# First stage of a two-layer diffusion trunk: order of the first loads, who scales the token rows, and which modulation tiles go to TensorE

## The chip, the cores and the metric

The kernel runs on one core of a Trainium2 chip. The metric is the device time of one execution in microseconds (us). The comparison time is the median of three runs.

## What is computed

The reference is a trunk of two layers over 512 latent tokens and 256 context tokens, each 1024 wide. Layer 0 is grouped-query attention, layer 1 a pooling mixer, and each is followed by a gated ConvFFN. Only the opening of layer 0 matters here:

```python
sc, sc_ctx = silu(c), silu(c_ctx)
m  = sc     @ w_mod[0] + b_mod[0]     # 6 vectors of 1024: shift_m, scale_m, ...
mc = sc_ctx @ w_mod[0] + b_mod[0]
h  = rmsnorm(x,   g_pre) * (1 + scale_m)  + shift_m
hc = rmsnorm(ctx, g_pre) * (1 + cscale_m) + cshift_m
q, k, v = h @ w_qkv                   # context gives k and v only
```

Everything is float32 to float32 accuracy: each matmul is made of three products of a high and a low part.

## The kernel before, in words

The 1024 features are eight tiles of 128 (index j), the tokens are six tiles of 128 rows (two of context, then four of x).

**Tokens.** Lines 337 to 350: for each of the six token tiles, a DMA brings its rows, ScalarE squares them with a running sum (`rstd_row`, line 174), VectorE makes mean plus epsilon (157), GpSimd raises to the power -1/2 (151), and ScalarE multiplies the rows by the result (347). The normalised rows are `xn`.

**Modulation.** For feature tile j and v = 0 (shift) or 1 (scale), a 512 KB piece of `w_mod` lies with features on partitions. VectorE multiplies it by the row silu(c_ctx) and sums (line 329, result `cmods`), then by the row silu(c) (line 330, in place, result `mods`): four such products for each j. The rows silu(c) and silu(c_ctx) stand on every partition (`scrow`, `cscrow`) and come by a broadcast DMA and a Silu on ScalarE. Tile 5 (`PE_TILE`) is made on TensorE instead, with silu(c) as two columns (`cols`): sixteen matmuls give two rows of 256 (319), ScalarE copies these (320), two transposes turn them into columns (323), and VectorE adds the bias (324, 325). The pieces of w_mod go through four buffers in turn (`mraws`), so the fifth load waits for the first product pair.

**Loop over j** (lines 355 to 380). VectorE forms the gains `Acol` and `Acx` (359, 360). TensorE transposes tile j of the six `xn` into PSUM banks 7 (context) and 6 (x) (367). ScalarE applies gain and shift (370, 371). `split` (126 to 129) makes the high part by a ScalarE cast (128) and the low part by a VectorE subtraction (129): `hT` for x, `cT` for context, and, once for two j, `wkvh` and `wkvl` for the weights of k and v. Then eighteen matmuls (122 to 124) add the tile's share to six banks. The weights of v and k go through two buffers `raw`.

**After the loop** come the rotary tables (`fold_rope`, 387: a DMA into the slots of `cT`, then VectorE), the weights of q (`load_w`, DMA, cast, subtraction, into five pairs of buffers `whi` and `wlo`), 96 matmuls of q, `do_kv` for six token tiles, `q_done` and the attention.

**What sets the order.** The program is written as above and a planner puts the instructions of each engine into one fixed order when the program is built, by the place in the program and by what it expects to be ready. On the chip each engine runs its list in that order; a wait of one instruction holds all behind it. All DMAs are issued from one queue, that of SyncE (SP), in order too.

Of the kernel before, what the change touches and what calls it, by code (L numbers as in the profile page):

```python
# [11 lines left out]
F32 = mybir.dt.float32  # L12
F32R = mybir.dt.float32r
AF = mybir.ActivationFunctionType
ALU = mybir.AluOpType
AX = mybir.AxisListType

P = 128
D = 1024
SEQ = 512  # L20
CTX = 256
KT = D // P
TT = SEQ // P
CT = CTX // P
# [18 lines left out]
BW = BI + 2 * BE  # L43
NSLOT = 64

PE_TILE = 5


@with_exitstack
def trunk(ctx: ExitStack, tc: tile.TileContext, a, out: bass.AP):  # L50
    nc = tc.nc
# [17 lines left out]
    def bank(i):  # L69
        return bank_[i]  # L70
# [16 lines left out]
    def rows(name, i, n=2, dt=F32):  # L87
        return flat(slots(name, i, n, dt))
# [47 lines left out]
    def load_w(src, n, dst=None):  # L136
        raw = load_raw(src)
        if dst is None:
            hi = wp.tile([P, 1024], F32R, tag="whi", name="whi")
            lo = wp.tile([P, 1024], F32R, tag="wlo", name="wlo")  # L140
        else:
            hi, lo = dst
        split(hi, lo, raw)
        return tuple(z.rearrange("p (a b) -> p a b", a=n) for z in (hi, lo))

    def row_tile(name):
        return work.tile([P, D], F32, tag="row", name=name)
# [24 lines left out]
    def rstd_row(src, junk):  # L172
        ss = small.tile([P, 1], F32, tag="ss", name="ss")
        S.activation(junk, src, AF.Square, accum_out=ss)
        return rstd(ss, 1, D)
# [116 lines left out]
            done(t)  # L292


    crow = row_tile("crow")
    nc.sync.dma_start(out=crow, in_=a["c"][0].broadcast_to([P, D]))
    S.activation(scrow, crow, AF.Silu)
    nc.sync.dma_start(out=bmod, in_=a["b_mod"])
    nc.sync.dma_start(out=gcols, in_=a["gcols"])
    cscrow = rows("cscrow", 48)  # L300
    mraws = [rows(f"mraw{n}", i) for n, i in enumerate((54, 56, 58, 62))]
    first = [(v, j) for j in range(KT) for v in range(2)]
    pe_raw = []
    cols = small.tile([P, KT, 2], F32, name="cols", bufs=1)
    nc.sync.dma_start(out=cols, in_=a["ccols"])
    S.activation(cols, cols, AF.Silu)
    modrow = small.tile([2, 256], F32, name="modrow", bufs=1)

    def first_load():
        raw = mraws[-len(first) % 4]  # L310
        v, j = first.pop(0)
        if j == PE_TILE:

            nc.sync.dma_start(out=raw, in_=a["w_mod0"][v])
            pe_raw.append(raw.rearrange("p (k f) -> p k f", k=4))
            if v == 1:
                m = bank(7)[0:2, 256:512]
                for k in range(KT):
                    T.matmul(m, cols[:, k, :], pe_raw[k // 4][:, k % 4, :], start=k == 0, stop=k == KT - 1)
                S.copy(modrow, m)  # L320
                mc = bank(7)[:, 256:260]
                for w in range(2):
                    T.transpose(mc[:, 2 * w:2 * w + 2], modrow[:, w * P:(w + 1) * P], ident[0:2, 0:2])
                V.tensor_add(mods[:, 0, 0:2, j], mc[:, 0:4:2], bmod[:, 0, 0:2, j])
                V.tensor_add(cmods[:, :, j], mc[:, 1:4:2], bmod[:, 0, 0:2, j])
            return
        nc.sync.dma_start(out=raw, in_=a["w_mod"][0, v, j])
        bias = bmod[:, 0, v, j:j + 1]
        V.tensor_tensor_reduce(mjunk, raw, cscrow, 1.0, bias, ALU.mult, ALU.add, cmods[:, v, j:j + 1])
        V.tensor_tensor_reduce(raw, raw, scrow, 1.0, bias, ALU.mult, ALU.add, mods[:, 0, v, j:j + 1])  # L330

    ccrow = row_tile("ccrow")
    nc.sync.dma_start(out=ccrow, in_=a["c"][1].broadcast_to([P, D]))
    S.activation(cscrow, ccrow, AF.Silu)
    first_load()

    xnT = []
    for n in range(CT + TT):
        xn = rows(f"xn{n}", 16 + 2 * n)
        if n < CT:  # L340
            src = row_tile("cx")
            nc.sync.dma_start(out=src, in_=a["ctx"][n * P:(n + 1) * P, :])
        else:
            src = x[n - CT]
            nc.sync.dma_start(out=src, in_=a["x"][(n - CT) * P:(n - CT + 1) * P, :])
        r = rstd_row(src, xn)
        S.activation(xn, src, AF.Copy, scale=r)
        xnT.append(xn)
        if n % 2 == 1:
            first_load()  # L350

    cTs = [(slots(f"cT{n}", 44 + 2 * n, 2), slots(f"c32{n}", 52 + n, 1, F32)[:, 0, :CTX]) for n in range(2)]
    hh32 = h32.rearrange("p (n a) b -> p n (a b)", n=2)
    wkv = []
    for j in range(KT):
        while first and first[0][1] <= j + 1:
            first_load()
        js = slice(j, j + 1)
        V.scalar_tensor_tensor(Acol[:, 0, 0, js], mods[:, 0, 1, js], 1.0, gcols[:, 0, 0, js], op0=ALU.add, op1=ALU.mult)
        V.scalar_tensor_tensor(Acx[:, js], cmods[:, 1, js], 1.0, gcols[:, 0, 0, js], op0=ALU.add, op1=ALU.mult)  # L360
        if j % 2 == 0:
            i = 28 + 2 * j
            wkv.append(load_w(a["w_qkv"][2, j // 2], 2, (rows(f"wkvh{j}", i, dt=F32R), rows(f"wkvl{j}", i + 2, dt=F32R))))
        f = slice(j * P, (j + 1) * P)
        for n in range(CT + TT):
            tp = bank(7)[:, n * P:(n + 1) * P] if n < CT else bank(6)[:, (n - CT) * P:(n - CT + 1) * P]
# [628 lines left out]
def _layout(x, c, ctx, c_ctx, w_mod, b_mod, g_pre_mix, g_post_mix, g_pre_ffn, g_post_ffn,  # L995
# [11 lines left out]

        "w_mod": w_mod.reshape(2, D, 6, KT, P).transpose(0, 2, 3, 4, 1),

        "w_mod0": w_mod[0].reshape(2, 4, P, 6, KT, P)[:, :, :, :2, PE_TILE].transpose(0, 2, 1, 3, 4).reshape(2, P, 1024),  # L1010

        "b_mod": b_mod.reshape(2, 6, KT, P).transpose(3, 0, 1, 2),
        "g_q": g_q.reshape(1, HD),
# [34 lines left out]
```

## Time and profile before

| | us |
|---|---|
| median of three runs | 1059.87 (1058.87 to 1060.57) |
| profiled execution | 1057.91 |
| its span in the profile | 1056.1 |
| TensorE busy | 990.8 (94%) |
| VectorE busy | 747.5 (71%) |
| ScalarE busy | 512.9 (49%) |

The profiled execution is one run of its own; its span is the time from the first to the last recorded instruction, and 1.8 us lie around it. A busy engine is one with an instruction in flight, so a TensorE that is always busy need not be at its peak. The shares are means over stages that have different limits, so the opening stage is read by itself.

### The profile page before, as it was taken

The numbers are of one execution on the slowest core, as the hardware profiler recorded it, in microseconds if no ns is written. First come the engines' busy times: TensorE is split into PE (matmuls) and PEld (weight loads), VectorE is DVE, ScalarE is ACT, GpSimd is POOL, SyncE is SP. The second block draws the span as 40 slices with busy tenths as digits, with TensorE's granted clock in tenths as the row PEclk, the third lists the DMA queues.
The fourth block names the chain that finished last, engine by engine and source line by source line (L and its number), as shares of the span: only waits on it lengthen the run. The fifth ranks groups of instructions, "written<-read, shape, count | busy, mean of one in ns | idle before, by whom it ended". The sixth has DMA issues, their size and how long they took to land.

```text
span 1056.1 us, 14619 instructions
## 1 busy us (share of the span) xinstructions
PE 990.8 (94%) x5592; PEld 857.4 (81%) x5592; DVE 747.5 (71%) x1259; ACT 512.9 (49%) x989; POOL 37.4 (4%) x55
## 2 busy tenths in 40 slices
PE   0899799999979999999999999789999999999997
PEld 0667697888878888888888877788999999988885
DVE  3988788985799999554532336789799999982214
ACT  5658589955634333433321233565455555761111
POOL 2003000000000000000000001100000000000000
PEclk9999899999989999999999999899999999999999
DMA  8643422450389998223322461401223232052212
GB/s 321 195 153 96 152 93 101 157 164 19 102 291 331 335 319 296 100 100 100 100 88 93 159 194 58 160 20 61 68 93 110 91 120 81 21 170 92 98 60 80
DMA packets 40611, 143.71 MB, mean 136 GB/s; under 512 B 4906, under 2 KB 5338, under 8 KB 40540
## 3 DMA queue, kind: packets, MB, share of 16 engines
q1 hardware_dynamic: 40540, 142.77, 39.7%
q8 instruction: 44, 0.72, 0.3%
q14 instruction: 27, 0.22, 0.1%
HBM read 140.63 MB, written 2.12 MB: 135 GB/s over the span
## 4 chain that ended last, share of the span: by engine, by line
PE 75%; DVE 8%; ACT 7%; DMA 5%; issue 3%; POOL 2%; SPq 0%; DVEq 0%; ACTq 0%; POOLq 0%
PE b L122 16%; PE b L124 16%; PE b L123 16%; PE b L749 6%; PE b L751 5%; PE b L750 5%; DMA mraw<-in_w_mod 2%; POOL rr L151 2%; PE tp L541 1%; DVE wlo L129 1%; DVE mraw L186 1%; ACT whi L128 1%; DVE x L264 1%; DMA raw<-in_w_up 1%; PE sc L122 1%
## 5 line engine op out<-in xcount | busy, mean ns | idle before, releaser
L129 DVE TENSOR_TENSOR wlo<-raw,whi 128x1024 fp32r<-128x1024 f32 x105 | 128.2, 1222 | 161.3 <-ACT whi L128 161.0
L128 ACT CAST whi<-raw 128x1024 fp32r<-128x1024 f32 x105 | 110.3, 1053 | 214.7 <-PE b L124 108.3
L122 PE MATMUL b<-hT,whi 128*128 128x512 f32 (+1 forms) x480 | 174.2, 364 | 5.2 <-ACT hT L128 5.2
L123 PE MATMUL b<-hT,whi 128*128 128x512 f32 (+1 forms) x480 | 174.4, 364 | 0.6 <-DVE hT L129 0.6
L124 PE MATMUL b<-hT,wlo 128*128 128x512 f32 (+1 forms) x480 | 174.1, 363 | 0.0
L123 PE MATMUL b<-wlo,a 128*128 128x512 f32 x320 | 125.1, 391 | 0.3 <-DVE wlo L129 0.3
L122 PE MATMUL b<-whi,a 128*128 128x512 f32 x320 | 125.3, 392 | 0.0
L124 PE MATMUL b<-whi,a 128*128 128x512 f32 x320 | 124.9, 392 | 0.0
L122 PEld LDWEIGHTS b<-hT,whi 128*128 128x128 f32 x480 | 91.6, 192 | 19.2 <-ACT hT L128 5.7
L123 PEld LDWEIGHTS b<-hT,whi 128*128 128x128 f32 x480 | 91.7, 191 | 15.0 <-DVE hT L129 1.1
L186 DVE CUSTOM_DVE_ANT_0 mraw<-mraw,scrow,bmod 128x1024 f32<-128x1024 f32 x80 | 100.6, 1278 | 4.2 <-DMA mraw<-in_w_mod 4.1
L124 PEld LDWEIGHTS b<-hT,wlo 128*128 128x128 f32 x480 | 91.7, 191 | 13.8
L749 PE MATMUL b<-hT,whi 128*128 128x256 f32 x288 | 81.9, 284 | 0.1
L751 PE MATMUL b<-hT,wlo 128*128 128x256 f32 x288 | 81.5, 283 | 0.0
L750 PE MATMUL b<-hT,whi 128*128 128x256 f32 x288 | 81.4, 283 | 0.0
L151 POOL TENSOR_TENSOR rr<-rv,mhalf 128x1 f32<-128x1 f32 (+2 forms) x48 | 36.7, 767 | 1013.3 <-DVE rv L169 848.1
L123 PEld LDWEIGHTS b<-wlo,a 128*128 128x128 f32 x320 | 60.4, 189 | 13.4 <-DVE wlo L129 0.7
L122 PEld LDWEIGHTS b<-whi,a 128*128 128x128 f32 x320 | 60.3, 189 | 13.1 <-ACT h L209 0.3
L124 PEld LDWEIGHTS b<-whi,a 128*128 128x128 f32 x320 | 60.5, 189 | 12.5
L749 PEld LDWEIGHTS b<-hT,whi 128*128 128x128 f32 x288 | 55.2, 192 | 1.0 <-ACT gates L778 0.9
L750 PEld LDWEIGHTS b<-hT,whi 128*128 128x128 f32 x288 | 55.2, 192 | 0.0
L751 PEld LDWEIGHTS b<-hT,wlo 128*128 128x128 f32 x288 | 55.2, 192 | 0.0
(317 smaller groups left out, 2151.2 us busy)
## 6 DMA issues: line engine op xcount, KB each, us to landing
mraw<-in_w_mod SPq DMA_DIRECT2D x96, 512.0 KB, 4.9
raw<-in_w_up SPq DMA_DIRECT2D x52, 512.0 KB, 3.5
raw<-in_w_down SPq DMA_DIRECT2D x44, 512.0 KB, 3.4
upv<-in_w_up SPq DMA_DIRECT2D x18, 512.0 KB, 4.1
upg<-in_w_up SPq DMA_DIRECT2D x18, 512.0 KB, 3.5
raw<-in_w_qkv SPq DMA_DIRECT2D x12, 512.0 KB, 3.6
raw<-in_w_o SPq DMA_DIRECT2D x8, 512.0 KB, 3.7
x<-in_x SPq DMA_DIRECT2D x4, 512.0 KB, 9.2
```

The lines of the kernel that those rows point to most:

```text
L122: T.matmul(ps, lh, rh, start=first, stop=False)
L123: T.matmul(ps, lh, rl, start=False, stop=False)
L124: T.matmul(ps, ll, rh, start=False, stop=last)
L128: S.copy(hi, src)
L129: V.tensor_sub(lo, src, F(hi))
L151: G.tensor_tensor(r[:, :n], v, mhalf[:, :n], op=ALU.pow)
L186: V.tensor_tensor_reduce(raw, raw, scrow, 1.0, bias, ALU.mult, ALU.add, mods[:, i, v, j:j + 1])
L264: V.scalar_tensor_tensor(xc, row[:, HALVES[c]], r, xc, op0=ALU.mult, op1=ALU.add)
L541: T.transpose(tp[:, kt * P:(kt + 1) * P], p[:, (3 * n + kt) * P:(3 * n + kt + 1) * P], ident)
L749: T.matmul(ps, lhs[0], rhs[0], start=first and k == 0, stop=False, skip_group_check=True)
L750: T.matmul(ps, lhs[0], rhs[1], start=False, stop=False, skip_group_check=True)
L751: T.matmul(ps, lhs[1], rhs[0], start=False, stop=last, skip_group_check=True)
```

## The change

Six things change in the opening stage; nothing after it does.

- SyncE issues first the columns of c and the two small tables, then w_mod of tile 0, the six token tiles, the first weights of k and v, w_mod of tile 1, and only then the two broadcast rows of c, which now land directly in `scrow` and `cscrow` and get their Silu in place.
- VectorE, not ScalarE, multiplies the token rows by their scale.
- Tiles 0 and 1 are made on TensorE, tile 5 no longer. The piece of w_mod is now the stationary operand (128 x 128) and the two columns of silu(c), silu(c_ctx) the moving one, so the result comes out as columns; the ScalarE copy and the transposes go. It is 32 matmuls instead of sixteen and two transposes.
- The pieces of w_mod have sixteen buffers: four as before, ten of `whi` and `wlo`, `Grow`, and one row tile.
- VectorE's products for tile j + 2 stand in the program ahead of step j's gains and splits; before, it was tile j + 1.
- The loads of the weights of k and v stand at other places of the program.

```diff
-PE_TILE = 5
+PE_TILES = (0, 1)
+    def raw_buffer():
+        n = len(raws)
+        if n < 4:
+            return rows(f"mraw{n}", (54, 56, 58, 62)[n])
+        if n < 14:
+            tag = ("whi", "wlo")[n % 2]
+            return wp.tile([P, 1024], F32, tag=tag, name="mraw")
+        return Grow if n == 14 else row_tile("mraw")
...
+    def first_mods(j):
+        if j in PE_TILES:
+            mc = bank(7)[:, 256:260]
+            for v in range(2):
+                for k in range(KT):
+                    w = raws[j, k // 4].rearrange("p (k v f) -> p k v f", k=4, v=2)
+                    T.matmul(mc[:, 2 * v:2 * v + 2], w[:, k % 4, v, :], cols[:, k, :], start=k == 0, stop=k == KT - 1)
+            V.tensor_add(mods[:, 0, 0:2, j], mc[:, 0:4:2], bmod[:, 0, 0:2, j])
+            V.tensor_add(cmods[:, :, j], mc[:, 1:4:2], bmod[:, 0, 0:2, j])
+            return
+        for v in range(2):
+            raw, bias = raws[j, v], bmod[:, 0, v, j:j + 1]
+            V.tensor_tensor_reduce(mjunk, raw, cscrow, 1.0, bias, ALU.mult, ALU.add, cmods[:, v, j:j + 1])
+            V.tensor_tensor_reduce(raw, raw, scrow, 1.0, bias, ALU.mult, ALU.add, mods[:, 0, v, j:j + 1])
...
+    def normalise(n):
+        xn = rows(f"xn{n}", 16 + 2 * n)
+        r = rstd_row(src[n], xn)
+        V.tensor_scalar(xn, src[n], r, None, op0=ALU.mult)
+        xnT.append(xn)
...
-        S.activation(xn, src, AF.Copy, scale=r)
...
+    load_mods(0)
     for n in range(CT + TT):
+        load_x(n)
+    load_kv(0)
+    load_mods(1)
+    for n, row in enumerate((scrow, cscrow)):
+        nc.sync.dma_start(out=row, in_=a["c"][n].broadcast_to([P, D]))
+    first_mods(0)
+    for n in range(CT + TT):
+        normalise(n)
+    load_mods(2)
+    load_mods(3)
+    load_kv(1)
+    for row in (scrow, cscrow):
+        S.activation(row, row, AF.Silu)
+    first_mods(1)
+    first_mods(2)
+    load_mods(4)
+    load_mods(5)
...
     for j in range(KT):
-        while first and first[0][1] <= j + 1:
-            first_load()
+        if j == 1:
+            load_kv(2)
+            load_mods(6)
+        if j == 2:
+            load_mods(7)
+        if j == 3:
+            load_kv(3)
+        if 0 < j and j + 2 < KT:
+            first_mods(j + 2)
         js = slice(j, j + 1)
...
-        if j % 2 == 0:
-            i = 28 + 2 * j
-            wkv.append(load_w(a["w_qkv"][2, j // 2], 2, (rows(f"wkvh{j}", i, dt=F32R), rows(f"wkvl{j}", i + 2, dt=F32R))))
```

## Rows read from the trace of the kernel before

**Rows 1.** Stretches of the opening: stretch, its length, busy us by engine, clock, DMA.
```profile
0.00:31.00 31.00, 3.54 (x8) 1.38 (x8) 13.20 (x32) 18.01 (x25) 7.26 (x13) 1.00 0.71 274
31.00:66.00 35.00, 34.46 (x154) 25.33 (x155) 33.29 (x67) 16.93 (x29) 0.00 (x0) 1.00 0.62 202
66.00:77.50 11.50, 10.53 (x50) 7.91 (x49) 8.29 (x19) 7.00 (x12) 0.00 (x0) 1.00 0.55 184
77.50:100.00 22.50, 22.50 (x105) 18.25 (x105) 20.71 (x70) 18.08 (x91) 8.46 (x9) 1.00 0.23 70
```

**Rows 2.** The chain of work that ended last, opening: start, length, what.
```profile
15.13 1.54 POOL rr L151
...
16.69 1.15 ACT xn L347
...
31.35 1.22 PE b L122 x2
```

**Rows 3.** Timeline, ScalarE and VectorE: start, length, instruction, idle before and releaser.
```profile
7.17 1.06 ACT L334 ACTIVATE cscrow<-ccrow 128x1024 f32<-128x1024 f32 x1 [1.29 <-DMA ccrow<-in_c]
10.40 1.06 ACT L174 ACTIVATE xn<-cx 128x1024 f32<-128x1024 f32 x1 [2.17 <-DMA cx<-in_ctx]
...
12.87 1.28 DVE L329 CUSTOM_DVE_ANT_0 mjunk<-mraw,cscrow,bmod 128x1024 f32<-128x1024 f32 x1 [0.93 <-DMA mraw<-in_w_mod]
```

**Rows 4.** Timeline of VectorE inside the loop over j.
```profile
47.72 1.28 DVE L329 CUSTOM_DVE_ANT_0 mjunk<-mraw,cscrow,bmod 128x1024 f32<-128x1024 f32 x1
...
48.93 0.69 DVE L129 TENSOR_TENSOR hT<-h,hT 128x512 fp32r<-128x512 f32 x1
49.53 1.28 DVE L330 CUSTOM_DVE_ANT_0 mraw<-mraw,scrow,bmod 128x1024 f32<-128x1024 f32 x1
...
50.74 0.42 DVE L129 TENSOR_TENSOR cT<-c,cT 128x256 fp32r<-128x256 f32 x1
51.08 0.15 DVE L359 SCALAR_TENSOR_TENSOR Acol<-mods,gcols 128x1 f32<-128x1 f32 x1
...
51.22 1.22 DVE L129 TENSOR_TENSOR wkvl<-raw,wkvh 128x1024 fp32r<-128x1024 f32 x1
52.35 1.28 DVE L329 CUSTOM_DVE_ANT_0 mjunk<-mraw,cscrow,bmod 128x1024 f32<-128x1024 f32 x1
...
65.62 0.08 DVE L330 DVE_READ_ACCUMULATOR2_ANT mods<- 128x1 f32 x1
```

**Rows 5.** Timeline of TensorE, same loop.
```profile
53.47 2.75 PE L319 MATMUL b<-mraw,cols 128*2 128x256 f32 x12
...
61.71 0.60 PE L367 MATMUL b<-ident,xn 128*128 128x128 f32 x4
...
66.53 0.71 PE L367 MATMUL b<-ident,xn 128*128 128x128 f32 x5
...
75.83 0.72 PE L124 MATMUL b<-wkvh,hT 128*128 128x512 f32 x2 [0.97 <-DVE hT L129]
...
77.55 0.39 PE L124 MATMUL b<-wkvh,hT 128*128 128x512 f32 x1
```

**Rows 6.** Waits of VectorE from 31 to 66: total, times, longest.
```profile
DVE mods L324 <- PE b L323: 0.8, 1, 0.8
DVE cT L129 <- ACT cT L128: 0.5, 1, 0.5
DVE hT L129 <- ACT hT L128: 0.4, 1, 0.4
```

**Rows 7.** Line 241: a scaling of rows on VectorE, 512 wide: ns min/median/max.
```profile
L241 DVE TENSOR_SCALAR xn<-x,rr x6: 479/484/490, 259.7 to 277.1; 128x512 f32<-128x512 f32 x6
```

**Rows 8.** Line 367: weight loads of 128 columns: ns min/median/max.
```profile
L367 PEld LDWEIGHTS b<-ident,xn x48: 138/140/230, 13.9 to 71.8; 128*128 128x128 f32 x48
```

**Rows 9.** TensorE after an idle stretch in the attention: timeline.
```profile
119.60 0.57 PE L122 MATMUL sc<-kv,qT 128*128 128x512 f32 x1 [1.85 <-ACT p L528]
```

**Rows 10.** The stretch behind that gap; columns as in the first group.
```profile
120.00:122.00 2.00, 2.00 (x8) 1.71 (x7) 1.59 (x4) 1.93 (x4) 0.00 (x0) 0.50 0.78 252
```

More of the change, by code (lines that the diff above doesn't have):

```diff
@@ L292, in out_proj @@
             done(t)
-    crow = row_tile("crow")
-    nc.sync.dma_start(out=crow, in_=a["c"][0].broadcast_to([P, D]))
-    S.activation(scrow, crow, AF.Silu)
+    cscrow = rows("cscrow", 48)
+    cols = small.tile([P, KT, 2], F32, name="cols", bufs=1)
+    raws = {}
+    def raw_buffer():
[6 more added lines that the diff above has]
+        return Grow if n == 14 else row_tile("mraw")
@@ new lines, in load_mods @@
+    def load_mods(j):
+        for v in range(2):
+            raws[j, v] = raw_buffer()
+            src = a["w_mod0"][PE_TILES.index(j), v] if j in PE_TILES else a["w_mod"][0, v, j]
+            nc.sync.dma_start(out=raws[j, v], in_=src)
+    def first_mods(j):
[8 more added lines that the diff above has]
+            return
+        for v in range(2):
+            raw, bias = raws[j, v], bmod[:, 0, v, j:j + 1]
+            V.tensor_tensor_reduce(mjunk, raw, cscrow, 1.0, bias, ALU.mult, ALU.add, cmods[:, v, j:j + 1])
+            V.tensor_tensor_reduce(raw, raw, scrow, 1.0, bias, ALU.mult, ALU.add, mods[:, 0, v, j:j + 1])
@@ new lines, in trunk, with load_x, load_kv @@
+    src = [row_tile(f"cx{n}") for n in range(CT)] + x
+    def load_x(n):
+        nc.sync.dma_start(out=src[n], in_=a["ctx"][n * P:(n + 1) * P, :] if n < CT else a["x"][(n - CT) * P:(n - CT + 1) * P, :])
+    wkv = []
+    def load_kv(kk):
+        raw = load_raw(a["w_qkv"][2, kk])
+        i = 28 + 4 * kk
+        hi, lo = rows(f"wkvh{kk}", i, dt=F32R), rows(f"wkvl{kk}", i + 2, dt=F32R)
+        split(hi, lo, raw)
+        wkv.append(tuple(z.rearrange("p (a b) -> p a b", a=2) for z in (hi, lo)))
@@ L298, in trunk @@
+    xnT = []
+    def normalise(n):
[3 more added lines that the diff above has]
+        xnT.append(xn)
+    nc.sync.dma_start(out=cols, in_=a["ccols"])
     nc.sync.dma_start(out=bmod, in_=a["b_mod"])
     nc.sync.dma_start(out=gcols, in_=a["gcols"])
-    cscrow = rows("cscrow", 48)
-    mraws = [rows(f"mraw{n}", i) for n, i in enumerate((54, 56, 58, 62))]
-    first = [(v, j) for j in range(KT) for v in range(2)]
@@ L303, in trunk @@
-    pe_raw = []
-    cols = small.tile([P, KT, 2], F32, name="cols", bufs=1)
-    nc.sync.dma_start(out=cols, in_=a["ccols"])
-    S.activation(cols, cols, AF.Silu)
[L307 to L330, printed above, removed]
@@ L332, in trunk @@
-    ccrow = row_tile("ccrow")
-    nc.sync.dma_start(out=ccrow, in_=a["c"][1].broadcast_to([P, D]))
-    S.activation(cscrow, ccrow, AF.Silu)
-    first_load()
-    xnT = []
-    for n in range(CT + TT):
[L339 to L346, printed above, removed]
-        S.activation(xn, src, AF.Copy, scale=r)
-        xnT.append(xn)
-        if n % 2 == 1:
-            first_load()
+    S.activation(cols, cols, AF.Silu)
@@ L353, in trunk @@
     hh32 = h32.rearrange("p (n a) b -> p n (a b)", n=2)
-    wkv = []
     for j in range(KT):
-        while first and first[0][1] <= j + 1:
-            first_load()
+        if j == 1:
[7 more added lines that the diff above has]
+            first_mods(j + 2)
         js = slice(j, j + 1)
@@ L1008, in _layout @@
         "w_mod": w_mod.reshape(2, D, 6, KT, P).transpose(0, 2, 3, 4, 1),
-        "w_mod0": w_mod[0].reshape(2, 4, P, 6, KT, P)[:, :, :, :2, PE_TILE].transpose(0, 2, 1, 3, 4).reshape(2, P, 1024),
+        "w_mod0": w_mod[0].reshape(2, 4, P, 6, KT, P)[:, :, :, :2, list(PE_TILES)]
+        .transpose(4, 0, 2, 1, 3, 5).reshape(len(PE_TILES), 2, P, 1024),
         "b_mod": b_mod.reshape(2, 6, KT, P).transpose(3, 0, 1, 2),
```

## The prediction

> **What bounds the kernel now.** I read four views, from coarse to fine. The stretches first: they show whose engine is late where. Up to 31 us TensorE is nearly idle (3.54 us busy) while ScalarE has the most work, 18.01; from 31 to 66 both TensorE (34.46 of 35.00) and VectorE (33.29) are full; from 66 to 77.5 VectorE has air (8.29 of 11.50) and TensorE works off what is left; from there to 100 TensorE is full again [rows 1]. Then the chain of waits, which tells why TensorE starts late: the chain runs from token tile to token tile through ScalarE's square, GpSimd's power (up to 1.54) and ScalarE's scaling (1.15), since the scaling of one tile stands on ScalarE ahead of the square of the next, and the first matmul of k and v comes at 31.35 [rows 2]. So the opening has two bounds: a ScalarE and GpSimd chain to 31, then TensorE, with VectorE a hair behind it. The last matmul of the loop over j starts at 77.55 [rows 5]; behind it come q and the attention, which have no fixed date. What the loop's end gains, the kernel gains, unless the end of another engine is later.
>
> The timelines give the prices. A step of the loop costs TensorE 66.53 - 61.71 = 4.82 us [rows 5]. VectorE's costs are start to start: a product 48.93 - 47.72 = 1.21, the low part of x 49.53 - 48.93 = 0.60, of context 0.34, a pair of gains 51.22 - 51.08 = 0.14, the low part of a weight 52.35 - 51.22 = 1.13 [rows 4].
>
> **The loads.** The fourth 512 KB transfer had landed at 10.40 and the sixth at 12.87, so 1.24 us apiece, the queue being full [rows 3]. The same three small tables still stand ahead of these. After the change x's last tile is the eighth instead of the eleventh: 12.87 + 2 x 1.24 = 15.3. The row of c_ctx is the thirteenth: 21.5; its Silu takes 1.06 [rows 3]; the first piece of tile 2 is the fourteenth, 22.8. Hence VectorE's first product starts at 22.8, where it had started its third at 12.87 before. The later pieces come at twice the rate at which VectorE takes them (two pieces in 2.5 us, four products in 4.84), so with sixteen buffers no later product waits for a DMA. The small moves of the k and v loads on SyncE's queue cost nothing while that lead lasts; the third one waits for a `raw` buffer with tiles 6 and 7 behind it, but tile 6 lands by 12.87 + 19 x 1.24 = 36.4 and is due after sixteen products, past 42. Without the lead they would cost a transfer each, 1.24.
>
> **The token rows.** ScalarE's scaling, six of 1.15, goes [rows 2]; VectorE's is not in the trace at this width. Half the width took 0.48 [rows 7]: between that and twice it, 0.96; I take 0.96, the whole amount of work at the known rate. All six lie before 22.8, when VectorE has nothing else, so they cost nothing; uncovered they would be 5.8. The last tile is ready by 15.3 + 1.06 + 1.54 + 0.96 = 18.9, some 10 us before the old date. TensorE can begin step 0 near 21 instead of 31.35.
>
> **Modulation on TensorE.** Sixteen matmuls inside the old loop go: twelve took 2.75, so 3.7 in all, on the engine that was late [rows 5]. The 32 new ones each load 128 columns of weights and move two. No row has that shape; a load of 128 columns took 0.14 to 0.23 [rows 8], so 4.5 to 7.4, and less than nothing is not possible since none of it existed. I take 4.5, from the median. Tile 0's half runs when TensorE is idle, tile 1's at about 19 to 23, before TensorE has work for long; as shown next TensorE waits for VectorE in mid-loop, so they hide there. Two waits are new: VectorE's bias addition for tile 1 waits for these matmuls, with all products queued behind it (the pieces land at 19.1, the half takes 2.3 to 3.7, so it is done at 21.4 to 22.8, in time for 22.8); and step 0's context transposes, which write the same bank 7, wait for that addition, with no loss as long as TensorE has air. VectorE does four products less, 4.8.
>
> **Where VectorE becomes the bound.** Its products for j + 2 now stand in the program ahead of step j's splits. The old trace shows how the order turns out: behind the first product of a pair one or two other operations get in (the second of the pair works on the same piece in place), here hT; between pairs come operations that stand earlier in the program, or any when a piece is missing, as cT, the gains and a weight did before 52.35 [rows 4]. All seven pairs that began between 40 and 65 have something in between. With all pieces in place pairs follow without a gap, so hT of step j, needed by TensorE, ends up inside the last pair of tile j + 2. For hT of step 5 that is the second pair of tile 7. Ahead of it lie: 23 products, 27.8; cT of steps 0 to 4, 1.7; hT of 1 to 4, 2.4; three weights, 3.4; four pairs of gains, 0.6. From 22.8 that ends at 58.7, and hT itself (0.69) at 59.4. Then TensorE has steps 5, 6 and 7 before it: 3 x 4.82 = 14.5, so the loop ends at 73.9 where it ended at 77.8 (77.55 and one more matmul's 0.2). That is 3.9 us. Before 59 TensorE waits about 1.1 per step (VectorE gives a step every 4 x 1.21 + 0.60 + 0.34 + 0.14 = 5.9).
>
> VectorE's own waits in the old loop were 1.7: 0.8 for tile 5's transposes, which go, and 0.9 for ScalarE's casts [rows 6]. I charge 0.9 again (bounds 0 and 1.7). **Sum: 3.0 us off**, between 2.2 and 3.9. VectorE is not late behind it: its last product ends near 60.9 where it ended at 65.7 [rows 4], 4.8 earlier. The rotary tables keep their distance to the end of the loop, for they wait for cT's slots.
>
> **The numbers.** The profiled execution took 1057.91, of which the sum makes 1054.9. The median of the runs lies 1.96 above it: **1056.9**.
>
> **Rivals.**
>
> *A, the splits are not held back* (chance 0.15): the planner puts hT and cT of each step in as soon as they are ready. Then all but step 7 is done when the last product ends: 22.8 + 24 x 1.21 + 7 x 0.34 + 6 x 0.60 + 3.4 + 6 x 0.14 = 62.0; gain, cast (each at most the 1.06 of a row twice as wide, together 1.6 as an estimate), low part 0.7 and one step end at 69.1, so 8.7 off, 7.8 with the waits: 1052.1. For it: c's rows come late, and what is ready by then goes first. Against: the order seen above.
>
> *B, TensorE's clock* (0.20): steps 2 to 5 each begin after a gap. A gap of 0.97 [rows 5] left the clock at 1.00 [rows 1]; one of 1.85 [rows 9] was followed by 2.00 us at 0.50, which is 1.2 of 2.4 GHz [rows 10]. The gaps of 1.1 are nearer to the first, and in the earlier ones VectorE is late anyway; but if it falls before step 5, at least half of 2.00, 1.0, and if it lasts twice that, 2.0 are lost. With VectorE's full 1.7 of waits that leaves 0.2 to 1.2 of 3.9: 1059.1. [...]
>
> *C, one step more is left over* (0.20), the slower side: the places inside the pairs are few, two for each tile, and weights and gains compete for them. If hT of step 4 comes only where I have hT of step 5, TensorE has four steps from 59.4: 78.7, with 0.9 of waits 79.6, and a longer gap with it, so 1.0 for the clock: 80.6, 2.8 later than before: 1062.7. It decides from hT of step 4 later than 77.8 - 4 x 4.82 = 58.5; I have it one tile earlier, near 53.5. For it: fewer things ran ahead of the products in the old order than the places allowed.
>
> **Chances and range.** Forecast 0.45 (1056 to 1057.7), A 0.15, B 0.20, C 0.20. A measurement of this kernel can tell about 0.2%, 2.1 us, from no change. Faster takes A and most of the forecast: 0.55. B and the rest make 0.25 within it; C makes slower 0.20. The range reaches to A and to C, 1051.5 to 1063, with some of either outside.
>
> **What would show it.** In the changed profile: the last token scaled by 19; the first product at 22.8, later products without a DMA as releaser; hT of steps 2 to 5 about 5.9 apart, TensorE's waits there put down to VectorE or ScalarE; TensorE's clock in these; the last matmul on wkvh near 74.5. I am wrong if TensorE's waits go on beyond 60, if VectorE sits idle in mid-loop, or if the stretch between the end of the loop and the first scores grows.

## The result, and the profile after

| | before | after |
|---|---|---|
| median of the runs (five each) | 1059.87 (1057.46 to 1060.57) | 1063.17 (1061.10 to 1065.21) |
| ratio, 95% interval | | 1.0053 (1.0033 to 1.0072) |
| profiled execution, its span | 1057.91, 1056.1 | 1065.21, 1063.4 |
| last matmul on wkvh (end of the loop over j) | 77.55 | 87.44 |
| first exponential's table load | 117.26 | 126.29 |

The change makes the kernel slower by half a per cent. In the profile the loop over j ends 9.9 us later instead of 3 to 4 earlier. 9.0 of that is left at the first exponential, 7.3 at the end of the span. The profiled execution is the slowest of its five, so its dates are used for the opening and the ratio for the time.

The stretches, columns as in [rows 1]:

```profile
0.00:31.00 31.00, 16.72 (x72) 15.51 (x72) 7.87 (x22) 10.72 (x17) 4.05 (x13) 1.00 0.93 362
31.00:66.00 35.00, 26.05 (x93) 19.96 (x93) 28.69 (x55) 13.29 (x21) 0.00 (x0) 0.85 0.37 133
66.00:77.50 11.50, 10.32 (x51) 7.96 (x50) 10.90 (x26) 5.35 (x11) 0.00 (x0) 1.00 0.04 18
```

TensorE now works 16.72 before 31 us (3.54 in [rows 1]), but mostly on columns, and from 31 to 66, where it had 34.46, it has 26.05. VectorE, which was to be full from 22.8 on, has 7.87 before 31 where it had 13.20. Both engines wait in the stretch that the change was to fill. VectorE's timeline shows for what (start, length, instruction, idle before and releaser):

```profile
12.91 0.16 DVE L323 TENSOR_TENSOR mods<-b,bmod 128x2 f32<-128x2 f32 x1 [11.18 <-DMA x<-in_x]
...
13.25 0.15 DVE L157 TENSOR_SCALAR rv<-ss 128x1 f32<-128x1 f32 x1
...
21.68 0.75 DVE L350 TENSOR_SCALAR xn<-x,rr 128x1024 f32<-128x1024 f32 x1 [0.73 <-POOL rr L151]
...
32.14 0.16 DVE L323 TENSOR_TENSOR mods<-b,bmod 128x2 f32<-128x2 f32 x1 [6.92 <-PE b L322]
...
38.16 1.28 DVE L328 CUSTOM_DVE_ANT_0 mjunk<-mraw,cscrow,bmod 128x1024 f32<-128x1024 f32 x1 [1.84 <-ACT cscrow L371]
```

Three waits in a row. The bias addition of tile 0 stands ahead of the first token's `rv`; it is put down to a DMA, but it comes as TensorE's first column block ends (below). The bias addition of tile 1 waits for TensorE until 32.14. The first product then waits for a Silu on ScalarE and starts at 38.16, 15.4 later than forecast. TensorE's side:

```profile
5.92 6.96 PE L322 MATMUL b<-cols,mraw 128*128 128x2 f32 x32 [5.92 <-DMA mraw<-in_w_mod]
...
22.58 0.44 PE L395 MATMUL b<-ident,xn 128*128 128x128 f32 x1 [1.10 <-DVE xn L350]
22.82 1.71 PE L322 MATMUL b<-cols,mraw 128*128 128x2 f32 x8
...
26.99 5.11 PE L322 MATMUL b<-cols,mraw 128*128 128x2 f32 x24
...
33.39 0.63 PE L395 MATMUL b<-ident,xn 128*128 128x128 f32 x2
...
46.21 0.90 PE L395 MATMUL b<-ident,xn 128*128 128x128 f32 x6 [2.62 <-ACT h L398]
...
59.21 1.15 PE L395 MATMUL b<-ident,xn 128*128 128x128 f32 x4 [6.03 <-ACT h L398]
...
87.44 0.39 PE L124 MATMUL b<-wkvh,hT 128*128 128x512 f32 x1
```

The sixteen column matmuls that the program writes for a tile stand in the trace as 32 (each of these float32 matmuls is two passes here) and take 6.96. Tile 1's block stands behind the transposes of x for step 0, which follow the token chain, so it starts at 22.82; step 0's first transposes and matmuls break into it from 24.39 to 26.99, and it ends near 32.1. Behind it come step 0's context transposes, at 33.39. And ScalarE:

```profile
32.59 0.78 ACT L398 ACTIVATE h<-b,mods,Acol 128x512 f32<-128x512 f32 x1 [8.10 <-DVE Acx L391]
34.05 0.56 ACT L399 ACTIVATE c<-b,cmods,Acx 128x256 f32<-128x256 f32 x1 [0.69 <-PE b L395]
34.52 1.04 ACT L371 ACTIVATE scrow<-scrow 128x1024 f32<-128x1024 f32 x1
...
36.61 0.56 ACT L399 ACTIVATE c<-b,cmods,Acx 128x256 f32<-128x256 f32 x1 [0.76 <-PE b L395]
37.08 1.05 ACT L371 ACTIVATE cscrow<-cscrow 128x1024 f32<-128x1024 f32 x1
```

The two Silus on c's rows stand in ScalarE's list behind operations of steps 0 and 1 that wait for VectorE and TensorE. ScalarE itself is idle for 8.10 ahead of them.

One more order shows in mid-loop. VectorE again:

```profile
50.63 0.08 DVE L329 DVE_READ_ACCUMULATOR2_ANT mods<- 128x1 f32 x1
50.63 1.28 DVE L328 CUSTOM_DVE_ANT_0 mjunk<-mraw,cscrow,bmod 128x1024 f32<-128x1024 f32 x1
...
58.13 0.15 DVE L390 SCALAR_TENSOR_TENSOR Acol<-mods,gcols 128x1 f32<-128x1 f32 x1
...
60.68 0.69 DVE L129 TENSOR_TENSOR hT<-h,hT 128x512 fp32r<-128x512 f32 x1
...
68.40 0.69 DVE L129 TENSOR_TENSOR hT<-h,hT 128x512 fp32r<-128x512 f32 x1 [0.60 <-ACT hT L128]
...
74.31 0.68 DVE L129 TENSOR_TENSOR hT<-h,hT 128x512 fp32r<-128x512 f32 x1
```

Tile 3's last product is read out at 50.63. Its gain, 0.15 us of work, comes at 58.13, behind five products of tiles 4 and 5 and the low parts of a context tile and of a weight: products two tiles ahead in the program go ahead of the gains too. TensorE waits 6.03 for what hangs on that gain (its row at 59.21 above). The low part of step 4 comes at 68.40; four steps of 4.82 from there end at 87.7, which is the loop's end.

### The profile page after: what moved, and what is told of

Its sections match the earlier page's. It is cut to its first block, busy times and chain, and to the rows that moved or that the text cites. A ratio compares the mean times of both kernels' runs of the same rounds, so it can differ in the third digit from the quotient of the medians.

```text
span 1063.4 us, 14693 instructions
## 1 busy us (share of the span) xinstructions
PE 1004.1 (94%) x5638; PEld 871.7 (82%) x5638; DVE 746.3 (70%) x1259; ACT 505.6 (48%) x982; POOL 34.0 (3%) x55
## 4 chain that ended last, share of the span: by engine, by line
PE 72%; DVE 12%; ACT 6%; DMA 5%; issue 3%; POOL 1%; SPq 0%; DVEq 0%; POOLq 0%; ACTq 0%
PE b L122 16%; PE b L124 16%; PE b L123 16%; PE b L777 5%; PE b L778 5%; PE b L779 5%; DVE wlo L129 2%; POOL rr L151 1%; DMA mraw<-in_w_mod 1%; PE tp L569 1%; DVE mraw L186 1%; DVE x L264 1%; DMA upv<-in_w_up 1%; ACT whi L128 1%; DVE mjunk L328 1%
## 5 line engine op out<-in xcount | busy, mean ns | idle before, releaser
L124 PEld LDWEIGHTS b<-hT,wlo 128*128 128x128 f32 x480 | 92.1, 192 | 13.8
L151 POOL TENSOR_TENSOR rr<-rv,mhalf 128x1 f32<-128x1 f32 (+2 forms) x48 | 33.2, 693 | 1024.1 <-DVE rv L169 847.4
```

The lines of the kernel that those rows point to most:

```text
L124: T.matmul(ps, ll, rh, start=False, stop=last)
L151: G.tensor_tensor(r[:, :n], v, mhalf[:, :n], op=ALU.pow)
```

## The experiments

Theory T: the loss is the late first product, made by two waits in a row (the dear columns that hold tile 1's addition, and the Silus behind step 0). Beside it stand D, the rows of c just land late, and E, the products' place two tiles ahead starves TensorE (a rival of T, or a second cost). An edit can change the lists of other engines too, since the planner orders them anew; where that shows in a trace it is said. Ratios are against the kernel before, run beside each (labels are shortened to their first part); "first" is the first product's start on VectorE, "end" the last matmul on wkvh.

| kernel | edit to the changed kernel | first | end | ratio (95% interval) |
|---|---|---|---|---|
| before | | | 77.55 | 1 |
| after | none | 38.16 | 87.44 | 1.0053 (1.0033 to 1.0072) |
| x1 | Silus first | 30.06 | 80.73 | 1.0005 (0.9992 to 1.0018) |
| x2 | row form | 27.29 | 78.24 | 0.9977 (0.9964 to 0.9990) |
| x4 | Silus first, products early | 23.69 | 79.98 | 0.9992 (0.9979 to 1.0006) |
| x5 | tile 1 on VectorE | 27.68 | 84.81 | 1.0036 (1.0019 to 1.0053) |
| x6 | one tile ahead | 38.12 | 82.94 | 1.0027 (1.0013 to 1.0042) |
| x8 | row form, Silus first, late addition, one ahead | 28.28 | 77.52 | 0.9977 (0.9961 to 0.9992) |
| x9 | scaling on ScalarE | 34.19 | 84.67 | 1.0044 (1.0027 to 1.0060) |
| x10 | eight buffers | 35.53 | 85.44 | 1.0056 (1.0036 to 1.0077) |
| x11 | c's rows first | 35.77 | 86.97 | 1.0054 (1.0039 to 1.0070) |
| y1 | row form, Silus first, products early | 26.52 | 78.52 | 0.9985 (0.9970 to 1.0000) |
| y2 | as y1, one ahead | 27.24 | 75.40 | 0.9957 (0.9944 to 0.9971) |
| w1 | as x4, one ahead | 23.55 | 78.75 | 0.9983 (0.9969 to 0.9996) |
| w2 | Silus first, one ahead | 30.22 | 76.58 | 0.9977 (0.9965 to 0.9989) |
| y3 | before, scaling on VectorE | | 76.77 | 0.9976 (0.9961 to 0.9990) |

**What holds the first product.** x1 puts both Silus ahead of step 0 in ScalarE's list:

```diff
-        S.activation(row, row, AF.Silu)
+        silu = S.activation(row, row, AF.Silu)
...
-        S.activation(h1, bank(6), AF.Identity, bias=mods[:, 0, 0, js], scale=Acol[:, 0, 0, js])
-        S.activation(c32, bank(7)[:, :CTX], AF.Identity, bias=cmods[:, 0, js], scale=Acx[:, js])
+        with tc.issue_after(silu.ins):
+            S.activation(h1, bank(6), AF.Identity, bias=mods[:, 0, 0, js], scale=Acol[:, 0, 0, js])
+            S.activation(c32, bank(7)[:, :CTX], AF.Identity, bias=cmods[:, 0, js], scale=Acx[:, js])
```

> The changed kernel with one thing else: ScalarE's list has the two Silus of c's rows ahead of the first gain operation of the loop. Theory T (the late start of VectorE's products is made of two waits in a row: tile 1's columns on TensorE hold the bias addition to 32.1, and the Silus stand behind step 0 on ScalarE's list to 38.1): first product near 32.4 instead of 38.2, end of the loop over j near 82 instead of 87.8, 1057 to 1060 us. Rival D (c's rows themselves land late, being loaded last): the Silus begin no earlier than before, first product near 38, 1063.

Measured: VectorE of x1 around the first product,

```profile
29.64 0.16 DVE L323 TENSOR_TENSOR mods<-b,bmod 128x2 f32<-128x2 f32 x1 [6.12 <-PE b L322]
...
30.06 1.28 DVE L328 CUSTOM_DVE_ANT_0 mjunk<-mraw,cscrow,bmod 128x1024 f32<-128x1024 f32 x1
```

The product follows the addition, without a wait of its own: 8.1 earlier, the loop's end 6.7 earlier, and the ratio falls by 0.0048, nearly the whole loss. Of the 8.1, 5.6 are the Silu's wait; the other 2.5 come because the addition itself is earlier, step 0's matmuls no longer breaking into tile 1's block (22.77 to 29.6 in one piece). D falls: the second row had landed when its Silu began,

```profile
21.40 1.06 ACT L371 ACTIVATE cscrow<-cscrow 128x1024 f32<-128x1024 f32 x1 [0.20 <-DMA cscrow<-in_c]
```

The addition still waits 6.12 for TensorE. x2 takes that wait on:

```diff
...
-                    T.matmul(mc[:, 2 * v:2 * v + 2], w[:, k % 4, v, :], cols[:, k, :], start=k == 0, stop=k == KT - 1)
+            m = bank(7)[0:2, 256:512]
+            for k in range(KT):
+                w = raws[j, k // 4].rearrange("p (k f) -> p k f", k=4)
+                T.matmul(m, cols[:, k, :], w[:, k % 4, :], start=k == 0, stop=k == KT - 1)
+            S.copy(modrow, m)
             for v in range(2):
...
+                T.transpose(mc[:, 2 * v:2 * v + 2], modrow[:, v * P:(v + 1) * P], ident[0:2, 0:2])
```

> The changed kernel with tiles 0 and 1 made in the old form (two columns as weights, 256 wide rows moving, ScalarE copy, two transposes), all else as changed. Theory T: the columns cost 64 weight loads, 7.0 us for a tile; the old form costs 16 weight loads of two columns, about 4 to 6 us for a tile at the half clock of this stretch, so the bias addition for tile 1 comes at 27 to 29 instead of 32.1 and the first product at about 33; 1058 to 1061. If the form does not matter (TensorE's tile 1 is late because it stands behind the transposes of the token rows), the addition stays within 1.5 us of 32 and the time at 1063.

With the weights and the moving operand exchanged back, tile 1's addition comes at 26.87 and the first product at 27.29, earlier than the 33 that T gave; the loop ends at 78.24 and the kernel is faster than before. The edit is worth 0.0076, but it changed the lists too, and that this is the form's price is not shown. VectorE and ScalarE of x2:

```profile
9.89 0.15 DVE L157 TENSOR_SCALAR rv<-ss 128x1 f32<-128x1 f32 x1 [8.17 <-ACT xn L174]
...
12.94 0.15 DVE L327 TENSOR_TENSOR mods<-b,bmod 128x2 f32<-128x2 f32 x1
...
18.65 0.75 DVE L354 TENSOR_SCALAR xn<-x,rr 128x1024 f32<-128x1024 f32 x1 [0.73 <-POOL rr L151]
...
25.48 1.05 ACT L375 ACTIVATE cscrow<-cscrow 128x1024 f32<-128x1024 f32 x1
```

The first two `rv` now stand ahead of tile 0's addition, so the last token is scaled by 19.4 instead of 22.4; and the Silu of `cscrow` stands ahead of step 0's c, so it holds nothing. In the form itself there is next to nothing: from the start of tile 1's block to its addition x2 takes 6.9 (19.93 to 26.87), copy and transposes included, and x1 with its columns in one piece takes 6.9 too (22.77 to 29.64). What x2 has over x1, 2.8 at the first product, 2.5 at the loop's end and 0.0028 in the ratio, goes with the token chain, which ends 3.0 earlier; TensorE's matmuls behind the block are faster as well (0.40 long at 25.45, in x1 0.63 until 34.50), and no run parts the two.

x5 takes tile 1 off TensorE:

```diff
-PE_TILES = (0, 1)
+PE_TILES = (0,)
```

> The changed kernel with tile 1 on VectorE, only tile 0 as columns on TensorE. Theory T: nothing on TensorE is ahead of the products, so the first one comes at 23 to 25; four more products cost 4.8; end of the loop 77 to 81, 1055 to 1058. Rival D: first product 33 or later, 1063 or more.

The first product comes at 27.68, not 23 to 25, the Silus standing behind step 0's h there too (25.65 and 26.61). VectorE has four products more, and the loop ends at 84.81, not 77 to 81. x2, with the first product at nearly the same date, ends 6.6 earlier: tile 1's place on TensorE is worth having.

x4 asks whether the earliest first product is the best; it keeps the edit of x1 and moves tile 2's products ahead of tile 1's addition:

```diff
-    first_mods(1)
     first_mods(2)
+    first_mods(1)
...
+            with tc.issue_after(last_mod[2].ins) if j == 1 else ExitStack():
                 V.tensor_add(mods[:, 0, 0:2, j], mc[:, 0:4:2], bmod[:, 0, 0:2, j])
                 V.tensor_add(cmods[:, :, j], mc[:, 1:4:2], bmod[:, 0, 0:2, j])
```

> As with the Silus ahead, and VectorE's bias addition for tile 1 stands behind the four products of tile 2. Both waits are gone. Theory T: first product at 22.8 to 23.5, as the prediction had it, end of the loop 73 to 76, 1050 to 1054. Rival E (it is the program order with tile j + 2 ahead of step j that starves TensorE, whenever the products start): first product at 23, but the end of the loop stays beyond 78, 1058 or more.

The first product comes at 23.69, near the 22.8 of the prediction. Yet the end is only 0.75 earlier than in x1, and hT of step 4 comes at 60.52 as there (61.05). Of E's two signs the end beyond 78 came, the time of 1058 did not (1056.46). What is gained by 23.69 is lost again further on; w1 below shows where. With tile 1 as columns, a first product earlier than x1's 30.06 no longer brings an earlier end by itself.

**How far ahead the products stand.** x6 undoes that alone:

```diff
-        if 0 < j and j + 2 < KT:
-            first_mods(j + 2)
+        if 1 < j and j + 1 < KT:
+            first_mods(j + 1)
```

> The changed kernel with the products one tile ahead in the program (for tile j + 1 in step j) as before the change, and nothing else undone. Theory T (the late first product is what costs; the order of products against splits is second): the first product stays at 38.2, the 24 products then keep VectorE until 38.2 + 24 x 1.21 + splits, so the last matmul of the loop stays between 85 and 87.4 and the time within 1061 to 1063.5. Rival E (standing two tiles ahead starves TensorE of hT): hT of steps 4 and 5 comes some 5 us earlier, the last matmul of the loop near 82.5, the time near 1058.

The loop ends at 82.94, as E said, and the ratio falls by 0.0026, about half of what E gave (1058; it is 1060.53). VectorE of x6, to be held against the rows of after from 50.63 on:

```profile
50.58 0.08 DVE L329 DVE_READ_ACCUMULATOR2_ANT mods<- 128x1 f32 x1
...
52.12 0.16 DVE L390 SCALAR_TENSOR_TENSOR Acol<-mods,gcols 128x1 f32<-128x1 f32 x1
...
57.02 0.69 DVE L129 TENSOR_TENSOR hT<-h,hT 128x512 fp32r<-128x512 f32 x1
```

Tile 3 is ready at the same moment; its gain comes at 52.12 instead of 58.13 and the low part 3.7 earlier. E is a second cost beside T. w2 joins the two orders and leaves everything else of the change, the column form included:

> The changed kernel with both Silus ahead of step 0 and products one tile ahead, nothing else. If the two undone orders add up (each gave 4.5 to 6.7 at the loop's end by itself): last matmul near 76, the time near 1054. If VectorE's sum of work sets the end once it is busy from the first product on: 30.1 plus 49 to 51, so 79 to 81, the time near 1058 as with the Silus alone.

The end comes at 76.58 and the ratio is 0.9977: the two add up (0.0048 and 0.0026 are 0.0074; measured 0.0076). So the change's parts, with nothing but these two orders undone, make the kernel faster than before. Tile 1's addition still waits for the columns there and comes at 29.79, so this first wait of T's need not go for that. w1 does the same from x4:

> The column form of the change kept; both Silus ahead of step 0, tile 2's products ahead of tile 1's bias addition, products one tile ahead. Theory T with E (the dates of the first product and of hT decide, the price of the columns then hides): first product 23.7 as in x4_silu_and_adds, hT of steps 4 and 5 a tile earlier than there, last matmul near 75.5, the time near 1054. Rival (the dear columns are a loss in themselves, since step 1 waits for tile 1's addition near 30): last matmul near 79.5 as in x4_silu_and_adds, the time near 1057.

Here the rival is right: the end is 78.75. VectorE of w1:

```profile
23.55 1.28 DVE L330 CUSTOM_DVE_ANT_0 mjunk<-mraw,cscrow,bmod 128x1024 f32<-128x1024 f32 x1
...
37.38 1.22 DVE L129 TENSOR_TENSOR wkvl<-raw,wkvh 128x1024 fp32r<-128x1024 f32 x1 [4.72 <-ACT wkvh L128]
```

The early products run into a new wait of 4.72 (3.84 in x4): the cast of the next weights stands on ScalarE behind step 1's h, and step 1's transposes stand on TensorE behind tile 1's columns and step 0's matmuls, which come 0.43 apart there and 0.23 later on. That the columns are then a loss in themselves is the likely reading, but w1 does not part them from these slow matmuls. y1 and y2 put the row form into x4 and w1:

> The row form for tiles 0 and 1, both Silus ahead of step 0 on ScalarE, tile 2's products ahead of tile 1's bias addition; products two tiles ahead as in the change. The other eight kernels give a relation: with products two tiles ahead the last matmul of the loop comes 49.3 to 51.2 after the first product, except where the products were put ahead of tile 1's addition (56.3). Theory T (the first product's date decides, span about 51): first product at 22.8 to 23.7, last matmul at 74 to 75, the time near 1052. Rival C (pairs leave too few places, so an early start of the products only holds up hT): last matmul near 79, the time near 1056.

> As y1_row_form_products_early, but products one tile ahead of the step. Theory T with E: first product 22.8 to 23.7, hT one tile earlier in the list, the last matmul at 72 to 73.5 and the time near 1050 to 1051. If VectorE's sum of work alone counts from the first product on, it ends as y1. Rival C without E: 79 and 1056.

y1's end is 78.52: T's 74 to 75 is wrong and C's 79 is near, but both rested on a first product at 23, and it came at 26.52. From there to the end are 52.0, against T's 51, so y1 does not decide between them. The Silu of cscrow stood behind ScalarE's copy of `modrow`, which waits for tile 1's matmuls. ScalarE of y2 shows the same:

```profile
20.71 1.06 ACT L377 ACTIVATE scrow<-scrow 128x1024 f32<-128x1024 f32 x1 [3.27 <-DMA scrow<-in_c]
25.89 0.36 ACT L325 COPY modrow<-b 2x256 f32<-2x256 f32 x1 [4.12 <-PE b L324]
26.16 1.05 ACT L377 ACTIVATE cscrow<-cscrow 128x1024 f32<-128x1024 f32 x1
```

y2 with one tile ahead ends at 75.40, 3.1 earlier, and is the fastest of all, 0.43% below the kernel before. The expected 72 to 73.5 went with a first product at 23; it came at 27.24. The form is not the only difference from w1: y2's last token is scaled by 19.6 instead of 22.5, as in x2. x8 tried the row form with both Silus first and one tile ahead too, the products not early, and besides moved tile 0's addition behind the fourth token:

```diff
-    first_mods(0)
     for n in range(CT + TT):
         normalise(n)
+    first_mods(0)
...
+            with tc.issue_after(scaled[3].ins):
                 V.tensor_add(mods[:, 0, 0:2, j], mc[:, 0:4:2], bmod[:, 0, 0:2, j])
```

> Tiles 0 and 1 in the row form of before (columns of c as weights, rows of 256, ScalarE copy, two transposes); both Silus ahead of step 0 on ScalarE; the bias addition of tile 0 behind the fourth token scaling on VectorE; products one tile ahead. Theory T with E: the token chain ends near 20.5 instead of 22.4, tile 1's bias addition comes near 25, the first product by 26, hT of the steps a tile earlier than in the row form alone, the last matmul of the loop near 72 and the time near 1050. Theory T without E (order of products against splits is indifferent, VectorE's sum of work decides): the last matmul near 76.5, some 1.5 us ahead of the row form alone, the time near 1053.5. If the token chain and the order count for nothing: 78.2 and 1055, as the row form alone.

The loop's end is 0.7 earlier than in x2, at the same ratio: all three edits together count for next to nothing there, nearest to the third expectation. They do not show what the token chain is worth. In x2 the first two `rv` stood ahead of tile 0's addition already, and in x8 the token rows landed later (first square at 10.23, in x2 at 8.71; the reason was not tested), so its last token is scaled by 20.9, later than x2's 19.4. VectorE is busy for 35.00 of the 35 us from 31 to 66 in x8: in this stretch it has no wait left that an order could take away.

**The other parts.** x9 gives the scaling back to ScalarE, x11 loads c's rows first, x10 takes away half of the buffers, y3 puts the scaling on VectorE in the kernel before and changes nothing else:

```diff
-        V.tensor_scalar(xn, src[n], r, None, op0=ALU.mult)
+        S.activation(xn, src[n], AF.Copy, scale=r)
```

> The changed kernel with the scaling of the token rows back on ScalarE, nothing else. If the move to VectorE is worth what the chain of the kernel before says, the last token is ready near 28 instead of 22.4, step 0 and everything behind it follows, and the time is 5 us above the changed kernel, near 1068. Theory T: the changed kernel spends that lead in waiting for tile 1's columns and the two Silus, so the time is within 2 us of the changed kernel, 1061 to 1065; the first product lies between 33 and 40.

> The changed kernel with the two broadcast rows of c loaded, and their Silus made, ahead of w_mod and the tokens, nothing else. Tokens and w_mod land 2 x 1.24 = 2.5 later. Theory T: the Silus no longer stand behind step 0, so the first product follows tile 1's bias addition at once, near 33 to 35 (2.5 later than 32.3 at most), against 38.2; with the loop's end some 3 to 5 us earlier than in the changed kernel, the time is 1059 to 1060. Rival D (the rows' late landing is the cost): the first product at 25 (the landing of tile 2's first piece), the time near 1054. Rival (token order is what pays): 2.5 us slower than the changed kernel, near 1065.5.

> The changed kernel with eight buffers for the pieces of w_mod instead of sixteen, so tiles 4 to 7 are loaded when the buffers of tiles 0 to 3 are free. Theory T: every piece still lands before VectorE comes to it, since the first product starts at 38 and a tile takes VectorE 4.8; no change against the changed kernel, 1062 to 1064. Rival: the lead of the loads carries the loop; then VectorE waits for DMAs from tile 5 on, a transfer and its latency for each piece, and the time is 3 or more above, 1066.

> The kernel before with the one edit that the token rows are scaled by VectorE; loads, modulation and buffers as before. By the chain of the kernel before (scaling on ScalarE ahead of the next square) the tokens come some 3 us earlier and TensorE starts near 28 instead of 31.35; VectorE, with 33.3 of 35 busy in the loop, then sets the end, so 1 to 2 us are gained: ratio 0.998 to 0.999. Rival: VectorE's products and the landings hold the rows as ScalarE did, ratio 1.000.

x9: the last token is scaled by 27.6 instead of 22.4, and the time is no worse (1.0044 against 1.0053). As T says, the changed kernel spends that lead in waiting; step 0's matmuls come too late there to break into tile 1's block, so the addition comes at 30.02, earlier than in after. y3 gives the counterproof: in the kernel before, the same edit alone brings 0.24%, a little more than expected. TensorE of y3:

```profile
27.11 0.44 PE L367 MATMUL b<-ident,xn 128*128 128x128 f32 x1 [1.10 <-DVE xn L347]
...
30.02 1.22 PE L122 MATMUL b<-wkvh,cT 128*128 128x512 f32 x2 [0.48 <-ACT wkvh L128]
```

It starts at 30.02 instead of 31.35 [rows 2], not near 28, though its last token is 3.3 earlier (the last transpose at 27.11, before at 30.41). x11 refutes D again (first product 35.77, not 25) but also T's number: the end is 86.97, not 3 to 5 earlier, and the ratio is that of after. The first product follows tile 1's addition at once, but the addition is 3.3 later (35.42), the tokens having landed later. x10 is as T says: no product waits for a DMA, and the lead that sixteen buffers give is not used. Its first product and its loop's end are 2.6 and 2.0 earlier than in after, for a reason on TensorE's side (last section), and its ratio is that of after.

**The price of the columns.** w3 makes tile 1's sixteen column matmuls once more in mid-loop, without using the result (one run, whose time is not compared):

```diff
+        if j == 5:
+            mc = bank(7)[:, 256:260]
+            for v in range(2):
+                for k in range(KT):
+                    w = raws[1, k // 4].rearrange("p (k v f) -> p k v f", k=4, v=2)
+                    T.matmul(mc[:, 2 * v:2 * v + 2], w[:, k % 4, v, :], cols[:, k, :], start=k == 0, stop=k == KT - 1)
```

> The changed kernel with tile 1's sixteen column matmuls made a second time inside the loop, ahead of the transposes of step 4 or 5, with the same operands; the second result is not used. It prices the disputed term where TensorE has been busy. If 0.217 us for each of the 32 passes belongs to the shape at any clock, the block takes 6.96. If the opening's half level doubles it, the block takes 3.5 here, 0.22 for each matmul, inside the bounds of the prediction (0.14 to 0.23); 2.3 would be the prediction's own price.

TensorE's timeline in w3, then the weight loads of line 394 in w3 and of line 322 in after (ns: min/median/max of one):

```profile
66.93 3.63 PE L394 MATMUL b<-cols,mraw 128*128 128x2 f32 x32
...
70.42 0.74 PE L401 MATMUL b<-ident,xn 128*128 128x128 f32 x5
```

```profile
L394 PEld LDWEIGHTS b<-cols,mraw x32: 190/192/192, 66.8 to 70.3; 128*128 128x128 f32 x32
```

```profile
L322 PEld LDWEIGHTS b<-cols,mraw x64: 287/333/365, 5.9 to 31.7; 128*128 128x128 f32 x64
```

The block takes 3.49 where the same block took 6.96 in the opening: 0.22 a matmul against 0.44. Each of the two passes loads its own 128 columns of weights. So the price has two factors: the shape in mid-loop, 0.22 for the two passes, which lies inside the prediction's bounds (0.14 to 0.23), and a factor of two in the opening, which does not.

## Why the prediction was wrong, point by point

The forecast was 1056.9 and faster; the kernel is at 1063.17 and slower. The step that failed is "Two waits are new": tile 1's addition was to be done in time for a first product at 22.8, and step 0's wait for it was to cost nothing. The addition came at 32.14 and the first product at 38.16. Of these 15.4, 9.3 lie ahead of the addition (the columns, their place, and step 0's matmuls among them) and 6.0 behind it (the Silus).

- **Landings: right.** The row of c_ctx was given for 21.5; x1's Silu waits for it until 21.40. Where nothing else held the first product it started at 23.55 (w1) and 23.69 (x4), right behind a weight's low part on VectorE. Later products waited for no DMA.
- **Token rows: price right, date wrong.** VectorE's scaling takes 0.75 (bounds 0.48 to 0.96). But "when VectorE has nothing else" was false: tile 0's addition stood ahead of the first `rv` until 12.91, and the last token came at 22.4 instead of 18.9. I had named the new wait for tile 1 and missed the same one for tile 0. In x2, where the first two `rv` stand ahead of it, the last token comes at 19.4, and its loop's end is 2.5 earlier than x1's, which was not shown to come from that alone.
- **Columns: the term that was mis-sized.** 4.5 us for 32 matmuls; measured 6.96 + 1.71 + 5.11 = 13.8. Two unlike things were counted: the program writes 32 new matmuls, which are 64 passes in the trace, while the sixteen of the old form are passes already (the program writes eight). In passes it is 64 instead of sixteen. The rows of the price, [rows 8], are single passes of float32 transposes; the new matmuls are two passes each, and the opening runs them at half the rate of the loop. A pass in mid-loop took 0.109 (w3), less than the 0.14 of [rows 8], so that two of them fall inside the bounds for one is luck. Also their place: I had tile 1's block at 19 to 23, "before TensorE has work for long". It starts at 22.82, behind the transposes that wait for the last token.
- **"With no loss as long as TensorE has air": the wait that cost most.** I named the context transposes that wait for tile 1's addition, and did not follow the wait one engine on: ScalarE's c stands behind them, and the Silus stand behind c. From the addition at 32.14 to the first product at 38.16 that is 6.0; x1 took away this wait (and the 2.5 of step 0's matmuls) and with it most of the loss.
- **VectorE as the bound: right, from the wrong start.** From first product to loop's end I had 51.1 (22.8 to 73.9); measured 49.5 (38.16 to 87.7). The low part of step 5 stands inside the last pair of tile 7, as said (74.31). The last steps are 5.9 apart (68.40, 74.31). So the whole miss at the loop's end, 13.8, is the first product's 15.4 less 1.6.
- **Behind the loop** nothing was to change. Of 9.9 us at the loop's end 7.3 are left at the end. The kernels with the new loads take 934 to 938 us from the first exponential on, before and y3 939. One place is the wait ahead of the second group of scores, 1.85 in [rows 9] and 1.07 after; the rest is spread out, and why was not tried. So one execution's date for the loop's end does not stand for the time: x9's is 2.8 earlier than in after and x10's 2.0, at 1.0044 and 1.0056.

**The rivals.** A (splits not held back) named the wrong operation: step 3's low part does come soon after its cast (59.51, 60.68), but the gain ahead of both was held until 58.13. B (the clock): TensorE's gaps of 2.62 and 6.03 were followed by a granted clock of 0.50 (48 to 50, 59.2 to 64), but both lie before step 4, where VectorE is late anyway; as far as the trace shows, what can hang on them is at most the 0.60 for which VectorE waits ahead of 68.40. C came out near the time (1062.7), by luck, with hT of step 4 at 68.40, later than its 58.5, and the loop's end is four steps from there. But its cause, too few places, is not what made after slow: in x1 the first product alone took 6.7 off. Where the products do start early (x4, w1) little is gained by it either, but by another wait than C's. The order two tiles ahead, on which C rests, has a price. The 51.1 of the sum held it, so it is no part of the miss, but I never set it against one tile ahead, which gives 0.0026 to 0.0028 in three of four pairs (after to x6, x1 to w2, y1 to y2; x4 to w1 0.0009).

The Trainium skill, in "TensorE: Matmul & The Clock Gate", section "Loop structure matters more than you think", says that a long DMA wait between matmuls makes TensorE go cold. The gap of 6.03, a wait for ScalarE, agrees (granted clock 0.50 behind it).

## What to carry to other kernels

A wait that a change adds has to be followed through every engine's list until it ends: here it went from TensorE's columns to VectorE's addition, back to TensorE's transposes, to ScalarE's gain and shift, and only then to the Silu for which all products waited. Work that is moved "into idle time" must be priced in the passes that a trace counts, at the rate which the engine has there, and at its place in that engine's list, not at the time when its data land. Preparing work further ahead also puts it ahead of the tiny operations which the next step needs: 0.15 us of gain waited 7.5 us, most of it behind products. And an edit that seems to change one thing can reorder the lists of other engines: x2 was to price a form, and it moved the token chain and the Silus as well.

## What the runs showed of the hardware that was not expected

TensorE's granted clock column doesn't tell everything about its rate. The stretches of the two column blocks, after and w3, and the stretch behind the gap of 6.03 in after:

```profile
5.92:12.88 6.96, 6.95 (x32) 6.87 (x32) 0.00 (x0) 4.29 (x7) 0.00 (x0) 1.00 1.02 417
```

```profile
66.93:70.42 3.49, 3.49 (x34) 3.49 (x33) 3.01 (x6) 2.54 (x4) 0.00 (x0) 1.00 0.03 11
```

```profile
59.20:64.00 4.80, 4.79 (x13) 3.70 (x14) 4.80 (x10) 3.12 (x5) 0.00 (x0) 0.50 0.00 0
```

The first two have 1.00 and the same 32 passes, and one takes twice the other. The matmuls of 512 columns say which is which, in after:

```profile
26.13 0.63 PE L122 MATMUL b<-wkvh,hT 128*128 128x512 f32 x1
...
38.33 0.40 PE L124 MATMUL b<-wkvh,cT 128*128 128x512 f32 x1
...
61.62 0.63 PE L122 MATMUL b<-wkvh,cT 128*128 128x512 f32 x1
```

0.63 is their length at 61.62, where the column reads 0.50, that is 1.2 of 2.4 GHz; at 26.13 it is 0.63 as well, under 1.00. So I read the opening as the lower level, unrecorded; a second cause that lengthens both by the same factor was not excluded. x10 has both rates in the opening. The 24 passes that take 5.11 in after take 2.87 there, behind the same matmuls of step 0, and the column reads 1.00 in both; from 31 to 34 it reads 0.52, and the matmuls of 512 columns are 0.63 long again:

```profile
27.41 2.87 PE L322 MATMUL b<-cols,mraw 128*128 128x2 f32 x24
```

```profile
27.41:30.28 2.87, 2.87 (x26) 2.87 (x25) 0.00 (x0) 0.00 (x0) 0.00 (x0) 1.00 0.81 331
31.00:34.00 3.00, 3.00 (x12) 2.41 (x11) 0.42 (x1) 2.26 (x5) 0.00 (x0) 0.52 0.92 291
```

So neither the shape nor its place in the list makes the dear rate. What the opening costs on TensorE is read from lengths, not from that column.

The Trainium skill, in "TensorE: Matmul & The Clock Gate", section "LDWEIGHTS (loading the stationary operand)", has the load's time go by the columns loaded, 107 ns for 128 by its formula. w3 agrees for each of its 32 passes (3.49 / 32 = 0.109), and the opening's 6.96 / 32 = 0.217 is twice that. So turning the matmul round to make its small side the moving one saved nothing here: 128 columns are loaded for two that move, and from the block's start to the addition both forms took 6.9 (x1, x2).
